# The first layer's up-projection by seven products of quarters, without the modulation vectors that nobody reads

## The chip, the cores and the metric

The kernel runs on one core of one Trainium2 chip, in one launch. The metric is the device time in microseconds (us). Five engines work side by side, each through its own list in its own order: TensorE (PE; the loads of its stationary operands are shown apart as PEld), VectorE (DVE), ScalarE (ACT), GpSimd (POOL) and SyncE (SP), which here issues the transfers of the weights. They wait for each other by semaphores.

## The reference, cut to what matters

Two layers of a transformer work on 512 tokens of x and 256 context tokens (ctx), 1024 features wide. Each layer has a mixer and then a feed-forward part, both behind a norm that is modulated by vectors computed from a conditioning vector, one set for x and one for ctx. After the second layer only x is returned, so that of ctx the second layer needs no more than what its mixer reads.

```python
hx = rmsnorm(x, g1) * (1 + sc1) + sh1          # and the same for ctx, with its own vectors
...                                            # mixer, output projection, gated residual
a, b = jnp.split(h @ w_up, 2, axis=-1)         # w_up: 1024 x 5632
return (jax.nn.silu(a) * b) @ w_down           # w_down: 2816 x 1024, then a gated residual
```

## The kernel before

Activations stand feature-major: a tile holds 128 features (partitions) by up to 768 tokens, x in columns 0 to 511 and ctx in 512 to 767. Every dense product of two float32 operands is made of three passes over float32r parts: each operand is split into a high part (a cast, on ACT, line 174) and a low part (operand minus high part, on VectorE, line 185); TensorE adds high·high, high·low and low·high. In the profile the tiles `whi` and `wlo` are the parts of weights, `act` the parts of activations, `t` temporaries, `main` and `bank` banks of PSUM.

**The up-projection.** The 22 feature tiles of the feed-forward part are taken in blocks (`F_BLOCKS`, line 27), six, six, six and four. The first two tiles of a layer come out of `Firsts` (line 725), which runs along with the norm, chunk by chunk of the contraction. For every other tile `f` the loop at line 1644 calls `dense_pass` (line 707) twice, for the half `a` that goes through silu and the half `b` that is multiplied: 8 chunks of contraction, three passes, once for 512 and once for 256 tokens. On layer 0 this is 96 matmuls a tile, 48 of 512 columns and 48 of 256. The result is taken out of PSUM by a silu on ACT and a product on VectorE, and split again, 512 and 256 wide. After each block comes the down-projection of its features, eight output tiles `m`, each added to the residual stream (`residual`).

**Weights** follow one list, `plan` (lines 350 to 489), which sets the order of loads, of splits and of uses. SP loads each item into one of four buffers `raw`. `w_next` (line 544) hands out the next item and lets `w_advance` (line 500) issue loads as buffers come free, and the split of the item ahead (cast and subtract, 1024 elements wide), into `whi` and `wlo`, two buffers each.

**Modulation items** stand in the same list. Those for the second half of layer 0's vectors and all of layer 1's are computed on VectorE beside dense products: `mod_step_v` (line 660) takes one item, two rows of 512 columns, by four instructions, two rows for each of x and ctx, and adds them up in two accumulators; after four items, two transposes, two reduces, a small product and an addition finish 512 modulation values for both. On layer 0 one item follows each half of each feature tile, one each down tile of the first three blocks, and two stand at the start of the feed-forward part, behind its first two tiles. The output projection's second half, `tail` at line 1594 with keys `o2` (the name in the list), has none.

**What sets the order.** Each engine runs its list in the order in which the program writes it; a rough clock per engine (`Plan`) decides where side chains (the norm, the transposes and reduces of modulation) are put between the main chain's instructions. `S.mm`, `S.tt`, `S.stt`, `S.acopy`, `S.act` are lines 136, 185, 196, 174 and 152; a profile's row names the helper's line.

Of the kernel before, what the change touches and what calls it, by code (L numbers as in the profile page):

```python
# [39 lines left out]
# a run of tokens: first, end, which modulation (x or ctx)  # L40
# [5 lines left out]
# column layout of the constant table  # L46
# [3 lines left out]
# column layout of the transposed small vectors  # L50
# [3 lines left out]
# column offsets of w_in  # L54
# [3 lines left out]
# fwd and bwd order of the 128-token tiles; tiles 4 and 5 are ctx  # L58
# [31 lines left out]
class Plan:  # L90
    """Keeps a rough clock per engine, so that independent chains of work are
    issued in an order in which the tensor engine seldom waits."""
# [33 lines left out]
    # -- the engines --  # L126
    def mm(self, out, lhsT, rhs, start, stop, tile_position=None):
# [7 lines left out]
        kw = {} if tile_position is None else dict(tile_position=tile_position)  # L135
        self.pin("pe", self.nc.tensor.matmul(out, lhsT, rhs, start=start, stop=stop, **kw))  # L136
# [5 lines left out]
    def behind(self, ins, other):  # L142
        # on one engine: the order of issue alone
# [15 lines left out]
    def preload(self):  # L159
        # one table that has both Exp and Ln  # L160
# [58 lines left out]
    # -- room in PSUM and SBUF, by the rough clock --  # L219
# [10 lines left out]
    def free(self, owner=None):  # L230
        # what is kept for a group of chains is free for that group alone
# [22 lines left out]
    # -- chains of work beside the main one --  # L254
# [62 lines left out]
def hybrid_kernel(ctx: ExitStack, tc: tile.TileContext, x, c, cx, c_ctx, w_mod, b_mod, norm1_g, norm2_g,  # L317
# [10 lines left out]
    # banks of PSUM: for the dense products, and for the chains beside them  # L328
# [22 lines left out]
    def w_item(key, n, load, width=P, hold=False):  # L351
        plan.append(dict(key=key, n=n, load=load, width=width, hold=hold, mod=False, early=False, read=False, late=False,
                         apart=False))

    # on the tensor engine up to the second norm, on the vector engine beside the first feed-forward part
# [3 lines left out]
    def mod_items(n):  # L359
        for _ in range(min(n, len(mod_todo))):  # L360
# [5 lines left out]
            else:  # L366
# [3 lines left out]
                             early=False, read=False))  # L370

    def first_mods(k):
        # shift and scale of the first norm, for the features of chunk k
# [80 lines left out]
    for l in range(DEPTH):  # L454
# [17 lines left out]
        for bi, (f0, f1) in enumerate(F_BLOCKS):  # L472
# [1246 lines left out]
```

## Time and profile before

| what | us |
|---|---|
| median of 3 runs | 1659.12 (1658.52 to 1661.16) |
| the profiled execution's span, first to last instruction | 1655.9 |
| time in it from which the output projection `o2` runs | about 390 |
| start of the up-projection's tiles after the first two | about 462 |
| end of layer 0's feed-forward part | about 981 |

The profiled execution's own time from outside is not listed; its span lies 3.2 us under the median of the runs. Rows of a window of the trace give, in this order, the stretch, its length, the busy time (and number of instructions) of PE, PEld, DVE, ACT and POOL, the granted clock as a share of full speed, the share of the 16 DMA engines and GB/s. Rows of a timeline give the start, the busy time of one row or of a run of equal ones, engine, line, operation, output and inputs, shapes and the count; a bracket at the end names the idle time ahead of it and what ended it. As instructions overlap at their ends, the pace of a stream is read from start to start, and not from the busy time.

### The profile page before, as it was taken

The page shows a single profiled execution, that of the slowest core. Times are in us where ns is not written, and L with a number is a line of the kernel's source. Part 1 is how long each engine was busy: PE and PEld are TensorE (multiplying, and loading weights), DVE is VectorE, ACT ScalarE, POOL GpSimd, SP SyncE. Part 2 cuts the span into 40 slices and gives each one's busy share as a digit, 9 for nine tenths or more (in the row PEclk, how much of TensorE's full clock was granted, in tenths as well). Part 3 has the DMA queues.
Part 4 walks back from the last instruction along what each step waited for, and adds up shares of the span by engine and source line. Part 5 has one row for each costly group of instructions (what it writes and reads, how often), then busy time and mean ns, then how long its engine had stood idle before and what let it go on. Part 6 is the DMA issues. An engine that isn't in the chain of part 4 may idle for free.

```text
span 1655.9 us, 26996 instructions
## 1 busy us (share of the span) xinstructions
PE 1619.7 (98%) x11021; PEld 1371.7 (83%) x11026; DVE 1056.2 (64%) x2016; ACT 598.7 (36%) x1194; POOL 35.7 (2%) x58
## 2 busy tenths in 40 slices
PE   7999999999999999999999999998999999999998
PEld 5878778888888888888888888786889888888887
DVE  5687877669867766767752366879787533333336
ACT  4454544543422122112212235555474422223224
POOL 2000000000000000000000000000000000000002
PEclk9999999999999999999999999999999999999999
DMA  9830312244234544444442152201123233232322
GB/s 259 253 100 15 90 52 77 83 160 138 67 115 124 145 125 121 138 128 140 127 118 71 33 146 52 64 27 52 65 77 90 77 89 106 83 117 84 100 85 77
DMA packets 252540, 168.45 MB, mean 102 GB/s; under 512 B 29700, under 2 KB 232960, under 8 KB 252416
## 3 DMA queue, kind: packets, MB, share of 16 engines
q1 hardware_dynamic: 248832, 155.93, 32.8%
q0 software_dynamic: 1760, 5.47, 1.1%
q10 hardware_dynamic: 1824, 5.31, 0.9%
q8 instruction: 87, 1.43, 0.4%
q14 instruction: 37, 0.30, 0.1%
HBM read 159.35 MB, written 7.34 MB: 101 GB/s over the span
## 4 chain that ended last, share of the span: by engine, by line
PE 83%; DVE 8%; ACT 2%; issue 1%; DMA 0%; SPq 0%; DVEq 0%; ACTq 0%
PE main L136 69%; PE bank L136 11%; DVE act L185 3%; PE bank L140 3%; DVE t L185 1%; DVE t L213 1%; ACT t L152 1%; DVE mx L204 1%; DVE wlo L185 1%; ACT t L174 0%; DVE t L190 0%; DMA raw<-in_w_mod_dram 0%; DVE t L196 0%; DVE t L1140 0%; DVE act L196 0%
## 5 line engine op out<-in xcount | busy, mean ns | idle before, releaser
L136 PE MATMUL main<-act,whi 128*128 128x512 f32 (+1 forms) x4160 | 1131.1, 357 | 1.3 <-ACT act L152 1.3
L136 PEld LDWEIGHTS main<-act,whi 128*128 128x128 f32 x4160 | 731.8, 189 | 115.2 <-issue 9.1
L136 PE MATMUL main<-act,wlo 128*128 128x512 f32 (+1 forms) x2080 | 735.8, 354 | 1.7 <-DVE wlo L185 1.7
L136 PEld LDWEIGHTS main<-act,wlo 128*128 128x128 f32 x2080 | 393.0, 189 | 57.5 <-issue 2.7
L174 ACT CAST whi<-raw 128x1024 fp32r<-128x1024 f32 (+3 forms) x194 | 189.9, 979 | 486.7 <-PE main L136 455.6
L185 DVE TENSOR_TENSOR wlo<-raw,whi 128x1024 fp32r<-128x1024 f32 (+3 forms) x194 | 219.4, 1131 | 181.7 <-ACT whi L174 178.9
L196 DVE SCALAR_TENSOR_TENSOR t<-raw,cst,t 128x512 f32<-128x512 f32 x210 | 148.3, 746 | 40.9 <-DMA raw<-in_w_mod_dram 40.5
L196 DVE SCALAR_TENSOR_TENSOR act<-main,mods,act 128x512 f32<-128x512 f32 (+1 forms) x160 | 97.8, 614 | 96.5 <-PE main L136 95.4
L185 DVE TENSOR_TENSOR t<-main,t 128x256 f32<-128x256 f32 (+1 forms) x73 | 43.9, 601 | 110.2 <-PE main L136 106.8
L174 ACT CAST act<-t 128x512 fp32r<-128x512 f32 (+3 forms) x102 | 61.0, 599 | 124.8 <-DVE t L185 124.3
L152 ACT ACTIVATE t<-bank,nm 128x256 f32<-128x256 f32 (+1 forms) x144 | 69.7, 496 | 60.2 <-DVE nm L196 55.5
L136 PE MATMUL main<-act 128*128 128x256 f32 (+1 forms) x576 | 88.6, 311 | 0.0
L136 PEld LDWEIGHTS main<-act 128*128 128x128 f32 x576 | 79.9, 191 | 6.1 <-issue 0.3
L185 DVE TENSOR_TENSOR act<-t,act 128x512 fp32r<-128x512 f32 (+5 forms) x110 | 73.6, 672 | 12.7 <-ACT act L174 10.5
L136 PE MATMUL bank<-act,whi 128*128 128x256 f32 (+3 forms) x336 | 74.9, 298 | 0.0
L152 ACT ACTIVATE t<-main 128x512 f32<-128x512 f32 x69 | 36.2, 525 | 88.9 <-PE main L136 88.7
L136 PE MATMUL bank<-act 64*64 64x64 f32 (+2 forms) x608 | 62.7, 273 | 3.6 <-DVE act L185 3.4
L185 DVE TENSOR_TENSOR act<-act 128x768 f32<-128x768 f32 (+7 forms) x84 | 64.7, 782 | 1.3 <-ACT t L174 1.1
L204 DVE TENSOR_REDUCE mx<-bank 128x2 f32<-128x512 f32 (+2 forms) x104 | 56.2, 561 | 14.2 <-PE bank L136 13.7
L140 PE MATMUL bank<-tab,t 128*128 128x128 f32 (+1 forms) x396 | 56.4, 277 | 4.1 <-DVE nm L196 1.7
L136 PE MATMUL bank<-t,t 128*64 128x128 f32 (+1 forms) x720 | 58.0, 283 | 1.7 <-DVE t L200 1.5
L136 PEld LDWEIGHTS bank<-act 64*64 64x64 f32 (+1 forms) x608 | 47.8, 161 | 12.9 <-issue 5.4
(133 smaller groups left out, 1208.7 us busy)
## 6 DMA issues: line engine op xcount, KB each, us to landing
raw<-in_w_mod_dram SPq DMA_DIRECT2D x92, 512.0 KB, 4.2
raw<-in_w_up_dram SPq DMA_DIRECT2D x80, 512.0 KB, 3.9
raw<-in_w_down_dram SPq DMA_DIRECT2D x48, 384.0 KB, 3.4
raw<-in_w_in_dram SPq DMA_DIRECT2D x26, 512.0 KB, 4.0
raw<-in_w_in_dram SPq DMA_DIRECT2D x16, 256.0 KB, 3.8
raw<-in_w_out_dram SPq DMA_DIRECT2D x16, 256.0 KB, 2.9
raw<-in_w_out_dram SPq DMA_DIRECT2D x32, 128.0 KB, 3.0
raw<-in_w_up_dram SPq DMA_DIRECT2D x16, 256.0 KB, 4.3
```

What stands on the lines that cost most here:

```text
L136: self.pin("pe", self.nc.tensor.matmul(out, lhsT, rhs, start=start, stop=stop, **kw))
L140: self.pin("pe", self.nc.tensor.transpose(out, in_, ident))
L152: ins = self.pin("act", self.nc.scalar.activation(out, in_, func, **kw))
L174: self.pin("act", self.nc.scalar.copy(out, in_))
L185: self.pin(eng, self._v(eng).tensor_tensor(out, a, b, op))
L196: self.pin(eng, self._v(eng).scalar_tensor_tensor(out, a, s, b, op0, op1))
L204: self.pin("dve", self.nc.vector.tensor_reduce(out, in_, AX.X, op))
L213: self.pin("dve", self.nc.vector.copy_predicated(out, mask, data))
```

## The change

For layer 0 the up-projection of tiles 2 to 21 is made by Winograd's form of Strassen's scheme. Its operands are cut in quarters: the weights by half (`a` in row 1, `b` in row 2) and by half of the contraction, `a11`, `a12`, `a21`, `a22`; the activations by half of the contraction and by half of the 768 tokens, `b11` to `b22`, 384 tokens wide. Seven products of quarters take the place of eight (table `SEVEN`); each is 4 chunks of contraction by three passes, 12 matmuls of 384 columns, and goes to PSUM in three banks, in which products that are added anyway share a bank. A `Unit` is one tile `f`: `make` forms the sums of weight quarters (four additions, three of them in the `raw` buffers themselves) and splits all seven operands, 512 elements wide each, and `after` takes the products out of PSUM and combines them. `run_units` sets the order; the product `p4` of a tile is run inside the next tile. Parts of weights are made at most four products ahead, in the four buffers that were `whi` and `wlo`.

The norm ahead of it, `Quartered`, keeps each chunk at full precision as well (one more ACT instruction for each) and makes sixteen differences of quarters, `t1` to `t4`, each split again. Layer 0's blocks become five (5, 5, 4, 4, 4 tiles), so there is one more round of eight down products. `Opened` starts a block's first two down products on all but their last tile of features, while that last tile is still being combined.

Modulation: of layer 1, from the third vector on, only x's are computed (`ni`), as nothing reads ctx's. The two items that stood at the start of the feed-forward part now follow the first tile of `o2`; the others are spread two to a feature tile up to the fourth tile and one after that, and by a table over the down tiles.

```diff
-F_BLOCKS = ((0, 6), (6, 12), (12, 18), (18, 22))
+F_BLOCKS = (((0, 5), (5, 10), (10, 14), (14, 18), (18, 22)), ((0, 6), (6, 12), (12, 18), (18, 22)))
...
+            if l == 0 and m == 0:
+                mod_items(2)
...
-            if l == 0 and bi == 0:
-                mod_items(2)
...
-                    if l == 0:
-                        mod_items(1)
...
+                if l == 0:
+                    mod_items(2 if f < 4 else 1)
...
-                if l == 0 and bi < len(F_BLOCKS) - 1:
-                    mod_items(1)
...
+                if l == 0 and bi < len(blocks) - 1:
+                    mod_items((0, 1, 2, 2, 1, 1, 1, 0)[m])
...
+            if at["split"] > i and plan[i]["quarters"] and not (it["mod"] or it["quarters"]):
+                break
...
     def mod_step_v(l, g, q):
+        ni = 1 if l == DEPTH - 1 and g >= 4 else 2
...
-            for a, i in zip(acc, range(2)):
+            for i, a in enumerate(acc):
...
+    class Opened:
...
+    class Quartered(Normed):
...
+        def split(self, name, kk, src):
+            hi, lo = self.at(name, kk)
+            S.acopy(hi, src)
+            S.tt(lo, src, hi.bitcast(F32), ALU.subtract)
...
+                S.act(full[:, t0:t1], full[:, t0:t1], AF.Identity, bias=B)
...
+        def differences(self, names):
...
+                    if name == "t1":
+                        d = h[:, left]
+                        S.tt(d, d, h[:, right], ALU.subtract)
...
+                    self.split(name, kk, d)
...
+    SEVEN = dict(p1=("a11", "b11", "v", True), p2=("a12", "b21", "q", True), p3=("s4", "b22", "r", False),
+                 p4=("a22", "t4", "v", False), p5=("s1", "t1", "r", True), p6=("s2", "t2", "v", False),
+                 p7=("s3", "t3", "v", False))
+    class Unit:
...
+        def make(self, name):
+            if self.raw is None:
+                mod_steps()
...
+            if name == "s1":
...
+                S.tt(src, R["a21"], R["a22"], ALU.add)
+            elif name == "s2":
+                S.tt(R["a21"], R["a11"], R["a21"], ALU.add)
+                src = R["a11"]
+                S.tt(src, R["a21"], R["a22"], ALU.add)
+            elif name == "s3":
+                src = R["a21"]
+            elif name == "s4":
+                src = R["a12"]
+                S.tt(src, R["a11"], src, ALU.add)
...
+            at["ring"] = 1 - at["ring"]
+            tag = ("whi", "wlo")[at["ring"]]
+            b = wp.tile([P, 1024], F32R, tag=tag, name=tag, bufs=2)
...
+            S.acopy(hi, src)
+            S.tt(lo, src, hi.bitcast(F32), ALU.subtract)
...
+            w_load()
+        def run(self, j):
...
+            hi, lo = self.parts.pop(wname)
+            for kk in range(4):
...
+                xh, xl = self.norm.at(xname, kk)
+                for i, (a, x) in enumerate(((hi, xh), (hi, xl), (lo, xh))):
+                    S.mm(pt, a[:, kk, :], x, first and kk + i == 0, kk == 3 and i == 2, more=not first)
...
+        def after(self, j, pt):
...
+            if j == "p1":
...
+                S.acopy(a1, pt)
+            elif j == "p2":
+                S.tt(a1, pt, a1, ALU.add)
...
+                S.act(a1, a1, AF.Silu)
+            elif j == "p5":
+                S.acopy(self.tb[:, :w], pt)
+            elif j in ("p3", "p6"):
+                if self.mid:
+                    S.tt(a2, pt, a2, ALU.add)
+                    S.act(a2, a2, AF.Silu)
+                else:
+                    S.acopy(a2, pt)
...
+            elif j == "p7":
+                S.tt(self.tb[:, :w], pt, self.tb[:, :w], ALU.add)
+            elif j == "p4":
+                S.stt(a1, pt, -1.0, a1, ALU.mult, ALU.mult)
...
+                S.stt(a2, self.tb[:, :w], -1.0, a2, ALU.mult, ALU.mult)
...
+                S.acopy(hi[:, :2 * w], self.ta[:, :2 * w])
+                S.tt(lo[:, :2 * w], self.ta[:, :2 * w], hi[:, :2 * w].bitcast(F32), ALU.subtract)
...
+    def run_units(units, made, then):
...
+            make += [(u, j) for j in ("p1", "p5", "p6", "p2", "p3", "p7", "p4")]
+            run += [(u, "p1"), (u, "p5"), *([(u - 1, "p4")] if u else []), (u, "p6")]
+            run += [(u, "p2"), (u, "p3"), (u, "p7")] if u < n - 1 else [(u, "p3"), (u, "p7"), (u, "p2")]
...
+            return i < 4 or make[i - 4] in ran
...
-                dense_pass([(m, *w_next(keys[m]), 0)], X, segs, ev_)
+                if m < len(opened):
+                    opened[m].close(ev_)
+                else:
+                    dense_pass([(m, *w_next(keys[m]), 0)], X, segs, ev_)
+                mod_steps()
...
+                run_units(units, 2, then)
...
+                opened = [Opened((0, *heads[0], 0), ts_, sg)]
+                opened.append(Opened((1, *w_next((l, "d", bi, 1)), 0), ts_, sg))
```

Three places show what moves in the engines' lists. The first is VectorE in `o2`. Output tiles of `o2` have their residual addition into `act_3941`, `act_3935` and so on, and the low part of the weights of tile m is the subtraction that reads `raw`; `t3` rows with `cst_144` are modulation. Before, the low parts of tiles 1, 2 and 3 (`act_4555`, `act_4596`, `act_4619`) follow one another:

```order
L196 SCALAR_TENSOR_TENSOR t3_4540<-raw_4453,cst_144,t3_4540 128x512
L196 SCALAR_TENSOR_TENSOR t3_4541<-raw_4453,cst_144,t3_4541 128x512
L185 TENSOR_TENSOR act_4555<-raw_4462,act_4555 128x512
L196 SCALAR_TENSOR_TENSOR act_3935<-main_4558,mods0_136,act_3935 128x512
L196 SCALAR_TENSOR_TENSOR act_3935<-main_4574,mods0_136,act_3935 128x256
L185 TENSOR_TENSOR act_4596<-raw_4542,act_4596 128x512
L209 STREAM_TRANSPOSE t3_4581<-t3_4291 128x512
L185 TENSOR_TENSOR act_4619<-raw_4549,act_4619 128x512
L204 TENSOR_REDUCE part_4539<-t3_4581 128x16
```

After, two modulation items (eight rows on `raw_4462` and `raw_4541`, with `raw_4462` now holding the first of them) stand between the low parts of tile 1 (`act_4553`) and of tile 2 (`act_4608`):

```order
L212 STREAM_TRANSPOSE t3_4579<-t3_4291 128x512
L199 SCALAR_TENSOR_TENSOR t3_4539<-raw_4462,cst_144,t3_4539 128x512
L188 TENSOR_TENSOR act_4553<-raw_4547,act_4553 128x512
L207 TENSOR_REDUCE part_4538<-t3_4579 128x16
L199 SCALAR_TENSOR_TENSOR t3_4540<-raw_4462,cst_144,t3_4540 128x512
L199 SCALAR_TENSOR_TENSOR t3_4539<-raw_4462,cst_144,t3_4539 128x512
L199 SCALAR_TENSOR_TENSOR t3_4540<-raw_4462,cst_144,t3_4540 128x512
L199 SCALAR_TENSOR_TENSOR t3_4539<-raw_4541,cst_144,t3_4539 128x512
L199 SCALAR_TENSOR_TENSOR t3_4540<-raw_4541,cst_144,t3_4540 128x512
L199 SCALAR_TENSOR_TENSOR t3_4539<-raw_4541,cst_144,t3_4539 128x512
L199 SCALAR_TENSOR_TENSOR t3_4540<-raw_4541,cst_144,t3_4540 128x512
L188 TENSOR_TENSOR act_4608<-raw_4550,act_4608 128x512
```

Eight rows now stand between the two low parts, a reduce and seven of the eight new modulation rows, and a transpose and the eighth stand ahead of tile 1's low part. Before, only tile 0's two residual additions stood between tile 1's and tile 2's.

The second place is VectorE early in the first block. Before, one feature tile needs the low parts of two weight items (`wlo`, 1024 wide), a product and a split for 512 and for 256 tokens, and the rest is modulation:

```order
L185 TENSOR_TENSOR t3_5248<-main_5323,t3_5248 128x512
L196 SCALAR_TENSOR_TENSOR t3_5383<-raw_5390,cst_144,t3_5383 128x512
L196 SCALAR_TENSOR_TENSOR t3_5382<-raw_5390,cst_144,t3_5382 128x512
L185 TENSOR_TENSOR act_5249<-t3_5248,act_5249 128x512
L185 TENSOR_TENSOR t3_5248<-main_5351,t3_5248 128x256
L196 SCALAR_TENSOR_TENSOR t3_5383<-raw_5390,cst_144,t3_5383 128x512
L185 TENSOR_TENSOR act_5249<-t3_5248,act_5249 128x256
L185 TENSOR_TENSOR wlo_5395<-raw_5317,whi_5394 128x1024
```

After, the same stretch holds the sums of weight quarters (`raw_5296`, `raw_5353`), subtractions of 512 for seven weight operands (out to `whi` or `wlo`, now one ring), the last differences of activations (`act_4938`, `act_4989`), the combination of the first tile (`t3_5290`, `main_5277`), and modulation's transposes and reduces:

```order
L188 TENSOR_TENSOR act_4938<-t3_5072,act_4938 128x384
L188 TENSOR_TENSOR raw_5353<-raw_5296,raw_5353 128x512
L212 STREAM_TRANSPOSE t3_5461<-t3_4540 128x512
L188 TENSOR_TENSOR raw_5296<-raw_5353 128x512
L207 TENSOR_REDUCE part_5378<-t3_5461 128x16
L199 SCALAR_TENSOR_TENSOR t3_5094<-t3_4990,t3_5094 128x384
L188 TENSOR_TENSOR whi_5448<-raw_5296,whi_5448 128x512
L199 SCALAR_TENSOR_TENSOR t3_5290<-t3_5318,t3_5290 128x384
L188 TENSOR_TENSOR act_4989<-t3_5094,act_4989 128x384
L188 TENSOR_TENSOR wlo_5505<-raw_5296,wlo_5505 128x512
L199 SCALAR_TENSOR_TENSOR t3_5290<-main_5277,t3_5290 128x384
L188 TENSOR_TENSOR raw_5296<-raw_5296 128x512
```

What were a few wide rows for a feature tile has become many narrower ones, and the norm's differences stand among them.

The third place is TensorE inside the first blocks. Before, a half's product is 8 chunks of 512 columns, then of 256 (here the end of one bank's 256 columns and the begin of the next bank's 512):

```order
L136 MATMUL main_5351<-act_5051,whi_5254 128x256 x2
L136 MATMUL main_5351<-act_5051,wlo_5255 128x256
L136 MATMUL main_5351<-act_5090,whi_5254 128x256 x2
L136 MATMUL main_5351<-act_5090,wlo_5255 128x256
L136 MATMUL main_5398<-act_4840,whi_5319 128x512 x2
L136 MATMUL main_5398<-act_4840,wlo_5320 128x512
L136 MATMUL main_5398<-act_4879,whi_5319 128x512 x2
L136 MATMUL main_5398<-act_4879,wlo_5320 128x512
```

After, every product is 384 wide: the second product of a tile (`bank_6308`), then the fourth of the tile before (`main_6173`), then the sixth (`main_6293`) and the second one by number (`bank_6370`):

```order
L139 MATMUL bank_6308<-act_5186,whi_6269 128x384 x6
L139 MATMUL bank_6308<-act_5306,whi_6269 128x384 x6
L139 MATMUL main_6173<-act_4852,whi_6228 128x384 x3
L139 MATMUL main_6173<-act_4898,whi_6228 128x384 x3
L139 MATMUL main_6173<-act_4938,whi_6228 128x384 x3
L139 MATMUL main_6173<-act_4989,whi_6228 128x384 x3
L139 MATMUL main_6293<-act_5324,wlo_6290 128x384 x6
L139 MATMUL main_6293<-act_5337,wlo_6290 128x384 x6
L139 MATMUL bank_6370<-act_5013,whi_6340 128x384 x3
L139 MATMUL bank_6370<-act_5031,whi_6340 128x384 x3
```

The previous tile's `p4` separates `p5` from `p6`, so that between `p6` and the following `p2` no other product stands.

More of the change, by code (lines that the diff above doesn't have):

```diff
@@ L546, in w_next @@
         assert it["key"] == key, (it["key"], key)
-        if at["use"]:
+        if at["use"] and not plan[at["use"] - 1]["quarters"]:
             plan[at["use"] - 1]["read"] = True
@@ new lines, in product_t, with there @@
+    def product_t():
+        if S.fits(dict(act=1)):
+            t = act_t(F32R)
+            return (t[:, 0], t[:, 1]), [t]
+        S.room(t3=2)
+        ts = [tmp(dt=F32R) for _ in range(2)]
+        return tuple(ts), ts
+    def run_units(units, made, then):
+        make, run = [], []
+        n = len(units)
+        for u in range(n):
+            make += [(u, j) for j in ("p1", "p5", "p6", "p2", "p3", "p7", "p4")]
+            run += [(u, "p1"), (u, "p5"), *([(u - 1, "p4")] if u else []), (u, "p6")]
+            run += [(u, "p2"), (u, "p3"), (u, "p7")] if u < n - 1 else [(u, "p3"), (u, "p7"), (u, "p2")]
+        run += [(n - 1, "p4")]
+        ran = set()
+        def there(i):
+            return i < 4 or make[i - 4] in ran
+        for r in run:
+            while made < len(make) and there(made):
+                v, j = make[made]
+                units[v].make(SEVEN[j][0])
+                made += 1
+            if made == len(make) and make[-4] in ran and make[-3] in ran:
+                then()
+                made += 1
+            units[r[0]].run(r[1])
+            ran.add(r)
+        if made == len(make):
+            then()
@@ L1637, in hybrid_kernel, with hook @@
                 evs = [swiglu(sil, act_t(F32R)) for sil in sils]
-                Firsts((l, "up"), (ga, gb)).run(norm, lambda i, s, pt: evs[i % 2]("ab"[i // 2], s, pt))
+                def hook():
+                    begin(range(2, f1))
+                if not last:
+                    diff = S.spawn(norm.differences(("t1", "t2", "t3")), prio=-1,
+                                   when=lambda: S.clk["pe"] if norm.done.get(gb, 0) == NK else None)
+                Firsts((l, "up"), (ga, gb)).run(norm, lambda i, s, pt: evs[i % 2]("ab"[i // 2], s, pt),
+                                                None if last else hook)
@@ L1639, in hybrid_kernel @@
                 S.gave(*sils)
+                if not last:
+                    S.spawn(norm.differences(("t4",)), prio=-1, when=lambda: diff["ready"] if diff["done"] else None)
+            if last:
                 X = norm.X()
-                mod_steps()
-            for f in range(max(f0, 2), f1):
-                S.room(t3=1, act=1)
-                sil = tmp()
-                ev_ab = swiglu(sil, act_t(F32R))
-                for nm in ("a", "b"):
-                    dense_pass([(nm, *w_next((l, nm, f)), 0)], X, sg, ev_ab)
-                    mod_steps()
-                S.gave(sil)
@@ new lines, in hybrid_kernel @@
+            if bi < len(blocks) - 1:
+                ev_d = lambda m, s, pt: residual(l, 5, pt, m, s)
+                for m in range(NK):
+                    if m < len(opened):
+                        opened[m].close(ev_d)
+                    else:
+                        w = (m, *w_next((l, "d", bi, m)), 0)
+                        if not last and m == NK - 1:
+                            begin(range(*blocks[bi + 1]))
+                        dense_pass([w], ts_, sg, ev_d)
+                    if m:
+                        mod_steps()
```

245 lines of the change are left out of this document (207 added, 38 removed).

## The prediction

> **What bounds the kernel now.** I read the page first: the busy times, and the chain that ended last by engine.
>
> ```profile
> span 1655.9 us, 26996 instructions
> PE 1619.7 (98%) x11021; PEld 1371.7 (83%) x11026; DVE 1056.2 (64%) x2016; ACT 598.7 (36%) x1194; POOL 35.7 (2%) x58
> PE 83%; DVE 8%; ACT 2%; issue 1%; DMA 0%; SPq 0%; DVEq 0%; ACTq 0%
> ```
>
> TensorE is busy for 98% of the span and carries 83% of the chain; VectorE has a third of its time left. An average hides stages, so the next view is the windows: the o2 and norm stage (384 to 462 us), 100 us of the up-projection, a down-projection, and the last stretch of layer 0's feed-forward part; then the waits of TensorE from 384 to 985 us, one row in all.
>
> ```profile
> 384.00:462.00 78.00, 76.81 (x453) 67.27 (x453) 65.70 (x122) 32.07 (x56) 0.00 (x0) 1.00 0.35 100
> 596.00:696.00 100.00, 100.00 (x596) 88.07 (x595) 66.94 (x106) 22.22 (x34) 0.00 (x0) 1.00 0.44 129
> 696.00:748.00 52.00, 52.00 (x311) 45.51 (x310) 38.62 (x62) 7.99 (x10) 0.00 (x0) 1.00 0.47 138
> 873.00:981.00 108.00, 108.00 (x623) 95.25 (x623) 41.91 (x62) 30.01 (x48) 3.41 (x7) 1.00 0.33 93
> PE bank L136 <- DVE t L185: 1.1, 1, 1.1
> ```
>
> In the stages that change TensorE never stands still, at a granted clock of 1.00. So matmul time taken out comes off the end, as long as the engines that feed it keep up. VectorE is the one to watch: 84% busy from 384 to 462 us, 67% in the up-projection. ACT (22%) and the DMAs (44%) have room.
>
> **What is removed.** The chain has the price of a feature tile, the timeline of TensorE that of one matmul.
>
> ```profile
> 595.77 33.55 PE main L136 x192
> 629.50 33.55 PE main L136 x192
> ...
> 385.88 0.63 PE L136 MATMUL main<-act,whi 128*128 128x512 f32 x2
> 388.62 0.40 PE L136 MATMUL main<-act,whi 128*128 128x256 f32 x2
> 390.06 0.63 PE L136 MATMUL main<-act,whi 128*128 128x512 f32 x2
> ...
> 267.80 0.51 PE L136 MATMUL bank<-act 128*128 128x384 f32 x2
> 268.15 0.23 PE L136 MATMUL bank<-trib,identb 128*128 128x128 bf16 x1
> ```
>
> 192 matmuls are two tiles, so a tile takes 33.55/2 = 16.78 us. Twelve matmuls of 512 run from 385.88 to 388.62 (0.228 each), twelve of 256 until 390.06 (0.120). Two of 384 take 268.15 − 267.80 = 0.35, 0.175 each, which is also the mean of 0.228 and 0.120. A tile by seven products is 84 of them: 14.70 us. Twenty tiles save 20 × (16.78 − 14.70) = **41.5 us**. The list of the changed kernel has 1680 matmuls of 384 more, 20 × 84, so the count is not in doubt.
>
> The Trainium skill, "TensorE: Matmul & The Clock Gate", section "Back-to-back issue gap", gives N/2.4 + 2.5 ns for a warm matmul of N columns alone. By that a tile would go from 15.6 us (48 of 512 and 48 of 256) to 13.65 (84 of 384), an estimated saving of 39 us in twenty; the rows lie about 12 ns above it at both widths, and the rows decide.
>
> **What is added on VectorE.** Its paces are read from start to start.
>
> ```profile
> 597.84 0.42 DVE L185 TENSOR_TENSOR t<-main,t 128x256 f32<-128x256 f32 x1
> 598.17 0.74 DVE L196 SCALAR_TENSOR_TENSOR t<-raw,cst,t 128x512 f32<-128x512 f32 x1
> 598.83 0.42 DVE L185 TENSOR_TENSOR act<-t,act 128x256 fp32r<-128x256 f32 x1
> 599.17 1.22 DVE L185 TENSOR_TENSOR wlo<-raw,whi 128x1024 fp32r<-128x1024 f32 x1
> 600.30 2.74 DVE L196 SCALAR_TENSOR_TENSOR t<-raw,cst,t 128x512 f32<-128x512 f32 x4
> ...
> 404.07 0.69 DVE L185 TENSOR_TENSOR t<-t,t 128x512 f32<-128x512 f32 x1
> 404.68 1.29 DVE L185 TENSOR_TENSOR act<-raw,act 128x512 fp32r<-128x512 f32 x2
> ```
>
> A two-operand row takes 0.33 at 256, 0.60 at 512 (404.07 to 404.68) and 1.13 at 1024; a modulation row 0.66 at 512. Between them by width: 0.47 for a two-operand row of 384, 0.87 for 768, 0.53 for a modulation-like row of 384. A tile needs four sums and seven low parts of 512 (11 × 0.60 = 6.6), three additions of 384 (1.4), two products (1.1) and the last subtraction (0.9): 9.9 us, where before two of 1024 and 0.60 + 0.33 twice made 4.1. One modulation item for both vectors is 4 × 0.66, with its share of transposes and reduces about 3.3 us; for x alone 1.6. By the order of the items, those for both end with the second block's down-projection. So a tile asks 13.2 us of VectorE's time in the second block and 11.5 in the last three, against 14.7 of TensorE's. On ACT seven casts of 512 at 0.62 and six rows up to 768 wide at no more than 0.93, by width, are under 10 us of 14.7:
>
> ```profile
> L174 ACT CAST act<-t 128x512 fp32r<-128x512 f32 x52 | 32.3, 621 | 109.7 <-DVE t L185 109.7
> ```
>
> The unread vectors take 56 modulation rows, 8 first rows, 8 transposes and 8 reduces off VectorE, about 50 us; since TensorE did not wait for it, this alone gains nothing, but it is the room in the last three blocks. The fifth block adds eight residual additions of each width (8 × 1.06 us) and no matmul; down stages then hold 40 of 42 us on VectorE in the first and 34 in the second. Both are hidden behind products; uncovered they would cost their 8.5 us.
>
> **Where TensorE will wait: o2.** Before, VectorE and TensorE stood like this:
>
> ```profile
> 392.77 0.74 DVE L196 SCALAR_TENSOR_TENSOR t<-raw,cst,t 128x512 f32<-128x512 f32 x1
> 393.43 0.69 DVE L185 TENSOR_TENSOR act<-raw,act 128x512 fp32r<-128x512 f32 x1
> 394.04 1.14 DVE L196 SCALAR_TENSOR_TENSOR act<-main,mods,act 128x512 f32<-128x512 f32 x2
> 395.09 0.68 DVE L185 TENSOR_TENSOR act<-raw,act 128x512 fp32r<-128x512 f32 x1
> ...
> 394.24 2.00 PE L136 MATMUL main<-act 128*128 128x512 f32 x8
> ```
>
> Tile 1's low part was done at 394.04, ahead of its product at 394.24. Now it comes behind tile 0's additions (until 395.09), a transpose and a modulation row, so at about 395.1 + 0.6 + 0.7 + 0.6 = 397.0, while the third matmul wants it at 394.7: 2.3 us. Tile 2's comes a reduce, seven modulation rows and itself later, 0.6 + 4.6 + 0.6 = 5.8 us, against a product of 12 × 0.228 = 2.7: another 3 us. Behind it VectorE is free again. I take **5 us**, with bounds 0, if VectorE comes to these rows early enough, and 8, all ten rows uncovered. The two loads moved ahead of o2's on SP cost nothing while the DMAs are at 35%.
>
> **Where it will wait: the first block.** The tiles began like this:
>
> ```profile
> 461.58 0.58 PE L136 MATMUL main<-act,whi 128*128 128x512 f32 x1
> ...
> 455.17 0.69 DVE L185 TENSOR_TENSOR t<-main,t 128x512 f32<-128x512 f32 x1 [3.45 <-ACT t L152]
> 459.77 1.22 DVE L185 TENSOR_TENSOR wlo<-raw,whi 128x1024 fp32r<-128x1024 f32 x1 [1.54 <-ACT whi L174]
> ```
>
> VectorE had 3.45 + 1.54 us to spare here, which the first operands and differences fill. From the first tile's first product to the third tile's, the new list gives VectorE 66 rows: 20 two-operand rows of 512 (12.0), 16 of 384 (7.5), 4 of 256 (1.3), one of 768 (0.9), 8 products of 384 (4.2), 10 modulation rows (6.6), 2 first rows (0.8), two transposes and two reduces (2.5) and a small one: 36 us. TensorE has 158 matmuls for it, 27.6 us. The difference, **8.4 us**, is a wait on low parts of weights. Bounds: 0 if the products could run ahead, which four part buffers forbid; 12 if the reduces also wait for their transposes.
>
> **The rest.** In the steady run the nearest hand-over is a12's: its part buffer comes free when the previous tile's p4 is done, and only p6 (12 × 0.175 = 2.1 us) lies between that and its use, for a cast of 0.62 and a subtraction of 0.6 to 0.7 that queue behind at most one other row. That leaves half a us. No row of before shows such a hand-over; the nearest is the one wait of 1.1 us above. With 17 steady hand-overs the bounds are 0 and 17 × 1.1 = 19 us; I take **4**, nearer to none, as the one row stands against forty tiles' halves without any.
>
> **Sum**, from the median 1659.1 (the profiled span lies 3.2 us below it, and what surrounds the span stays): 1659.1 − 41.5 + 5 + 8.4 + 4 = **1635 us**.
>
> **The rivals.** *The whole gain:* the waits are hidden by order; 1659.1 − 41.5 = 1617.6, up to 1627. For it: one wait row in 600 us; against: 36 us of rows over 27.6 of matmuls. 0.17. *More waits:* hand-overs and the first block at their upper ends, 8 + 12 + 19 = 39, so 1641 to 1657: 0.13, of which 0.03 lies within 0.2% of before. *384 columns at the pace of the weight load:*
>
> ```profile
> L136 PEld LDWEIGHTS main<-act,whi 128*128 128x128 f32 x4160 | 731.8, 189 | 115.2 <-issue 9.1 <-ACT act L152 1.9 <-DVE act L196 0.7
> ```
>
> At 0.189 a tile takes 15.9 us, the gain is 18 and the waits eat it: about 1659. Against it, 256 columns run at 0.120 under the same loads. 0.03. *Slower: VectorE sets the pace of every tile.* If rows of sums in the `raw` buffers, read and rewritten between loads, are drawn out so that a tile's rows come to 16.4 us instead of 13.2 and 11.5, TensorE waits 1.7 us in each of 20 tiles, 34 us, and the sum is 1659.1 − 41.5 + 13.4 + 34 = 1665. It decides from 28/20 = 1.4 us a tile, where the gain left by the two early waits is used up. For it: VectorE has only 1.5 us of room a tile in the second block; against: 67% busy without one wait. 0.11. *The clock falls back in a wait.* At the start TensorE waits and the clock does not:
>
> ```profile
> 0.00:10.00 10.00, 3.59 (x16) 3.14 (x16) 1.65 (x5) 3.98 (x7) 7.16 (x21) 1.00 0.74 220
> 30.00:60.00 30.00, 30.00 (x303) 24.92 (x301) 17.29 (x38) 10.19 (x19) 0.00 (x0) 1.00 0.86 218
> PE bank L140 <- DMA tab<-in_table_dram: 5.3, 1, 5.3
> ```
>
> After a gap of 5.3 us the granted clock is still 1.00. If it halved for some 3.4 us behind each of one to four longer gaps, the cost would be 2 to 7 us: 1637 to 1642. The Trainium skill, "TensorE: Matmul & The Clock Gate", section "Part 1: The HAM clock gate", has that rule (half rate after an idle window of about 3.4 us); this trace does not bear it out. 0.04.
>
> **How the numbers follow.** The forecast with waits of 10 to 24 us, 1627 to 1641, has 0.52. A measurement can tell about 0.2% from no change, 1655.8 to 1662.4. Faster: 0.52 + 0.17 + 0.10 + 0.04 = 0.83; same: 0.03 + 0.03 = 0.06; slower 0.11. The range goes from the whole gain to most of the case of more waits, 1617 to 1653, and leaves out some 0.19: 0.11 + 0.03 + 0.04 of the case of more waits + 0.01 below.
>
> **What would show it.** In the changed profile: tiles of about 14.7 us in blocks two to five and matmuls of 384 at 0.175; a wait of TensorE of about 5 us on low parts of o2 and of about 8 in the first block; VectorE some 90 us busier (20 × 5.8 for the tiles, 16 for the differences, 8.5 for the fifth block, less 50); no row of waits in the last three blocks. Wrong would be the forecast if weight parts are waited for in every tile, if 384 columns run slower beside this many other rows, or if the two early stages have no waits at all.

## The result and the profile after

| | us |
|---|---|
| before, median of 4 runs | 1658.82 (1657.87 to 1661.16) |
| after, median of 4 runs | 1633.98 (1632.20 to 1635.71) |
| ratio | 0.9848, 95% interval 0.9834 to 0.9862 |
| profiled execution after: its time, its span | 1632.85, 1630.9 |

The change makes the kernel 24.8 us faster; 1635 was forecast. First the page of the changed kernel, by the same three lines as before, and the waits of TensorE from the start of o2 to the end of layer 0's feed-forward part (engine, line and bank, who is waited for, total us, times, longest).

```profile
span 1630.9 us, 26988 instructions
PE 1586.0 (97%) x10786; PEld 1370.5 (84%) x10786; DVE 1149.9 (71%) x2212; ACT 681.1 (42%) x1374; POOL 35.8 (2%) x58
PE 79%; DVE 10%; ACT 2%; DMA 1%; issue 1%; SPq 0%; DVEq 0%; ACTq 0%
...
PE main L139 <- DVE wlo L188: 4.7, 4, 1.8
PE main L139 <- ACT act L177: 2.3, 2, 1.2
PE bank L139 <- ACT wlo L177: 2.2, 1, 2.2
PE main L139 <- DVE act L188: 1.5, 2, 1.0
PE main L139 <- ACT wlo L177: 1.1, 1, 1.1
PE bank L139 <- DVE wlo L188: 0.3, 1, 0.3
```

TensorE has 33.7 us less to do and VectorE 93.7 us more. Where one row of 1.1 us stood, six rows stand with 12.1 us, all of them on the parts of operands that VectorE and ACT make.

What a product costs is read from the timeline of TensorE in the third block:

```profile
682.90 2.24 PE L139 MATMUL main<-act,wlo 128*128 128x384 f32 x12
684.98 2.24 PE L139 MATMUL bank<-act,whi 128*128 128x384 f32 x12
```

Twelve matmuls of 384 take 2.08 us, 0.173 each; a tile of seven products is 14.56 us. The tile before, 48 × 0.228 + 48 × 0.120 = 16.7 us by its matmuls alone, had the small products of modulation besides (0.1 us of the chain's 16.78), which stay. Twenty tiles save 20 × (16.70 − 14.56), about 42.8 us. Of these 18.0 were given back. The places follow.

**o2**, TensorE and then VectorE:

```profile
395.92 0.73 PE L139 MATMUL main<-act 128*128 128x512 f32 x2 [1.21 <-ACT act L177]
397.15 2.99 PE L139 MATMUL main<-act 128*128 128x512 f32 x12 [0.49 <-DVE act L188]
401.25 0.73 PE L139 MATMUL main<-act 128*128 128x512 f32 x2 [1.11 <-ACT act L177]
402.98 4.23 PE L139 MATMUL main<-act 128*128 128x512 f32 x11 [0.99 <-DVE act L188]
...
396.41 0.69 DVE L188 TENSOR_TENSOR act<-raw,act 128x512 fp32r<-128x512 f32 x1
...
397.60 4.72 DVE L199 SCALAR_TENSOR_TENSOR t<-raw,cst,t 128x512 f32<-128x512 f32 x7
402.24 0.68 DVE L188 TENSOR_TENSOR act<-raw,act 128x512 fp32r<-128x512 f32 x1
```

The second tile's low part is done at 397.10 and the third's at 402.92, behind the seven modulation rows; TensorE waits 1.21 + 0.49 + 1.11 + 0.99 = 3.8 us. Two of these waits, 1.21 and 1.11 us, end with the cast of a high part on ACT, and the second of these casts had waited 2.52 us for its load: SP issues the rest of o2's weights from 391.75 us on, where the kernel before issued them in one run from 381.72 on. The low parts are done later still, so that VectorE's rows set the time here.

**The first block**, TensorE and two rows of VectorE:

```profile
483.94 0.61 PE L139 MATMUL bank<-act,wlo 128*128 128x384 f32 x2 [2.16 <-ACT wlo L177]
484.88 3.42 PE L139 MATMUL bank<-act,wlo 128*128 128x384 f32 x10 [0.33 <-DVE wlo L188]
500.45 0.62 PE L139 MATMUL main<-act,wlo 128*128 128x384 f32 x2 [1.05 <-ACT wlo L177]
502.85 2.02 PE L139 MATMUL main<-act,wlo 128*128 128x384 f32 x10 [1.78 <-DVE wlo L188]
...
496.81 5.38 DVE L199 SCALAR_TENSOR_TENSOR t<-raw,cst,t 128x512 f32<-128x512 f32 x8
502.11 0.68 DVE L188 TENSOR_TENSOR wlo<-raw,wlo 128x512 fp32r<-128x512 f32 x1
```

The waits of 5.3 us stand in the second tile (p5) and at the third tile's p1, whose low part follows eight modulation rows.

**The clock.** The windows of the two stretches:

```profile
400.00:420.00 20.00, 17.90 (x78) 13.98 (x78) 17.53 (x28) 8.69 (x13) 0.00 (x0) 0.91 0.66 195
480.00:500.00 20.00, 16.91 (x91) 15.35 (x89) 18.32 (x34) 8.15 (x17) 0.00 (x0) 0.91 0.21 66
```

The granted clock was 1.00 there before. In windows of 1 us it is 0.50 from about 402.7 to 406.1 and from 484.6 to 488.0: 3.4 us at half speed, each beginning within the second of two waits and costing up to 1.7 us. The rows above show it too: ten matmuls of 384 take 3.42 us at 484.88 and 2.02 at 502.85.

The second of these rows follows waits of 1.05 and 1.78 us, more than o2's last two, and yet no half clock follows it. The two stretches of half clock begin 81.9 us apart, 24 times 3.41. Windows of 3.41 us, counted from there, are these ahead of 402.66 and at the third tile's waits:

```profile
399.25:402.66 3.41, 1.62 (x6) 0.68 (x5) 3.41 (x6) 0.62 (x1) 0.00 (x0) 1.00 0.39 115
498.23:501.64 3.41, 1.78 (x9) 1.14 (x7) 3.41 (x6) 0.62 (x1) 0.00 (x0) 1.00 1.08 264
```

TensorE stands idle for 1.79 us in the first and for 1.63 in the second, as the border at 501.64 cuts the longer wait in two. Where a wait falls decides along with its length; the last section has the count over all profiles.

**The down stages.** At 746 us TensorE waits 1.7 us for a low part of the third tile's weights, at 841 1.0. VectorE, then the queue of loads:

```profile
746.33 0.49 DVE L193 TENSOR_SCALAR t<-raw,cst 128x512 f32<-128x512 f32 x1 [2.12 <-DMA raw<-in_w_mod_dram]
746.73 0.75 DVE L199 SCALAR_TENSOR_TENSOR act<-main,mods,act 128x512 f32<-128x512 f32 x1
747.39 0.68 DVE L188 TENSOR_TENSOR wlo<-raw,whi 128x512 fp32r<-128x512 f32 x1
...
741.20 1.94 SPq L519 DMA_DIRECT2D raw<-in_w_mod_dram  x2
```

VectorE has nothing to do, but its next row is a modulation row whose load was issued at 741.20 and has not landed; a residual addition and the low part are queued behind it.

### The profile page after: what moved, and what is told of

Read it like the earlier page. It is cut to its first block, busy times and chain, and to the rows that moved or that the text cites. A ratio compares the mean times of both kernels' runs of the same rounds, so it can differ in the third digit from the quotient of the medians.

```text
span 1630.9 us, 26988 instructions
## 1 busy us (share of the span) xinstructions
PE 1586.0 (97%) x10786; PEld 1370.5 (84%) x10786; DVE 1149.9 (71%) x2212; ACT 681.1 (42%) x1374; POOL 35.8 (2%) x58
## 4 chain that ended last, share of the span: by engine, by line
PE 79%; DVE 10%; ACT 2%; DMA 1%; issue 1%; SPq 0%; DVEq 0%; ACTq 0%
PE main L139 58%; PE bank L139 19%; DVE act L188 3%; PE bank L143 3%; DVE t L188 1%; DVE wlo L188 1%; DVE t L199 1%; ACT t L155 1%; DMA raw<-in_w_mod_dram 1%; DVE t L216 1%; ACT t L177 1%; DVE mx L207 1%; DVE t L193 0%; DMA raw<-in_w_out_dram 0%; ACT whi L177 0%
## 5 line engine op out<-in xcount | busy, mean ns | idle before, releaser
L139 PE MATMUL main<-act,whi 128*128 128x512 f32 (+2 forms) x2976 | 812.8, 364 | 1.8 <-ACT act L155 1.3
L139 PEld LDWEIGHTS main<-act,whi 128*128 128x128 f32 x2976 | 530.1, 189 | 83.7 <-issue 9.1
L139 PE MATMUL main<-act,wlo 128*128 128x512 f32 (+2 forms) x1728 | 547.3, 358 | 7.5 <-DVE wlo L188 6.5
L177 ACT CAST whi<-raw 128x1024 fp32r<-128x1024 f32 (+4 forms) x222 | 186.8, 841 | 426.8 <-PE main L139 357.8
L188 DVE TENSOR_TENSOR wlo<-raw,whi 128x1024 fp32r<-128x1024 f32 (+4 forms) x162 | 171.7, 1060 | 102.8 <-ACT whi L177 99.7
L139 PE MATMUL bank<-act,whi 128*128 128x384 f32 (+4 forms) x736 | 153.5, 319 | 0.0
L139 PE MATMUL bank<-act,wlo 128*128 128x384 f32 (+4 forms) x548 | 127.5, 328 | 2.5 <-ACT wlo L177 2.2
L139 PEld LDWEIGHTS bank<-act,whi 128*128 128x128 f32 (+1 forms) x736 | 124.5, 187 | 4.5 <-DVE whi L188 0.2
L139 PEld LDWEIGHTS bank<-act,wlo 128*128 128x128 f32 (+1 forms) x548 | 98.8, 189 | 6.1 <-ACT wlo L177 2.5
L139 PE MATMUL main<-t,whi 128*128 128x256 f32 (+1 forms) x296 | 74.3, 338 | 0.0
```

The source lines that it names most:

```text
L177: self.pin("act", self.nc.scalar.copy(out, in_))
L188: self.pin(eng, self._v(eng).tensor_tensor(out, a, b, op))
```

## The experiments

Each is timed together with the kernel before, on the same chip; the waits are from its profile. Stretches of half clock come and go from profile to profile also where an edit changes nothing (at 24 us the change has one and run 4 has none, at 500 us it is the other way round), at up to 1.7 us for each 3.4. So a difference of 2 to 3 us between two of the runs is weak by itself.

**1. The vectors dropped alone**, on the kernel before.

```diff
+        ni = 1 if l == DEPTH - 1 and g >= 4 else 2
...
-            for a, i in zip(acc, range(2)):
+            for i, a in enumerate(acc):
...
```

> The kernel before, with only the unread modulation vectors dropped: no product of quarters, blocks and places of items as before. Theory (TensorE did not wait for VectorE there, so 50 us less on VectorE are worth nothing by themselves): 1657 to 1660 us, the same as before. Rival (part of the gain of the change comes from the dropped vectors): 1653 us or less.

1659.13 us, ratio 1.0001 (0.9992 to 1.0010). VectorE is busy for 1011.4 us in the place of 1056.2 (44.8 less, where about 50 were estimated), and nothing is gained: TensorE did not wait for it.

**2. The vectors kept**, beside the seven products.

```diff
-        ni = 1 if l == DEPTH - 1 and g >= 4 else 2
+        ni = 2
...
-                ns = 1 if l == DEPTH - 1 and sc >= 2 else 2
+                ns = 2
```

> The changed kernel, but with the context's modulation vectors of layer 1 computed again from the third on, as before the change (about 50 us more on VectorE, none on TensorE). Theory (they are worth nothing while TensorE is the bound, but fill the down stages of the later blocks: eight items at 3.3 us and 13 us of other rows against 33.4 us of matmuls): the up-projection tiles of blocks three to five stay without waits at 13.2 of 14.6 us, and the down stages of the third and fourth block wait about 6 us each: 1644 to 1648 us. Rival (VectorE has room for them everywhere): 1633 to 1635 us. Second rival (the tiles wait too, as their rows come late by the order): above 1652 us.

1644.17 us, 10 us slower than the change. The waits of TensorE from 680 to 980 us, and the clock in two windows:

```profile
PE bank L139 <- DVE whi L188: 5.2, 2, 2.6
PE main L139 <- DVE wlo L188: 4.5, 6, 1.0
...
780.00:800.00 20.00, 18.29 (x102) 18.03 (x103) 18.09 (x31) 8.76 (x16) 0.00 (x0) 0.91 0.37 106
880.00:900.00 20.00, 17.84 (x92) 17.57 (x93) 17.24 (x31) 7.13 (x15) 0.00 (x0) 0.83 0.31 89
```

The time is as the theory had it, the place only half: 4.5 us in the down stages, 5.2 at the second product of the block behind each, and there the half clock besides. This profile also has half clock from 499 to 506 us, ahead of any row that the edit adds, so that not quite all of the difference is shown to be the vectors'. What is worth nothing alone is worth about 10 us beside the seven products.

**3. The two items put back** from o2 to the start of the feed-forward part.

```diff
-            if l == 0 and m == 0:
-                mod_items(2)
...
+            if l == 0 and bi == 0:
+                mod_items(2)
```

> The changed kernel, with the two modulation items that it has after the first tile of o2 put back to the start of the feed-forward part, behind the four weight loads of the first two tiles. Theory (VectorE's rows are the bound from the first up-projection tile to the third, and the eight rows cost their 5.3 us wherever TensorE has no cover for them): the wait of 3.8 us in o2 and the stretch of half clock behind it (1.7 us) go, and the waits in the first block rise from 6.0 us to about 11: 1632 to 1636 us, the same as the changed kernel. Rival (the wait in o2 is only a matter of place, and the start of the feed-forward part has room for the rows, as it had in the kernel before): the 5.5 us are simply gained, 1628 to 1629 us.

1628.37 us: the rival was right. The waits of TensorE from 389 to 980 us (one more is of 0.2 us); the window from the start of o2 to shortly behind the third tile's start, in the change (114 us) and here (107 us); and the window from the first tile's first product to the third tile's low part, in the change and here:

```profile
PE main L139 <- DVE wlo L188: 3.7, 4, 1.3
PE bank L139 <- ACT wlo L177: 3.6, 1, 3.6
PE bank L139 <- DVE t L188: 1.1, 1, 1.1
```
```profile
389.00:503.00 114.00, 104.89 (x594) 92.52 (x593) 105.05 (x197) 59.31 (x113) 0.00 (x0) 0.97 0.31 90
```
```profile
389.00:496.00 107.00, 100.95 (x582) 90.34 (x581) 102.60 (x196) 58.82 (x112) 0.00 (x0) 0.98 0.32 96
```
```profile
466.52:502.85 36.33, 31.02 (x169) 28.73 (x167) 34.63 (x66) 17.71 (x37) 0.00 (x0) 0.95 0.30 87
```
```profile
460.10:495.65 35.55, 30.66 (x169) 28.91 (x167) 35.52 (x68) 17.88 (x37) 0.00 (x0) 0.95 0.30 89
```

Within the first block the theory holds: VectorE is busy for all but 1.7 us of that stretch in the change and for all of it here. What it had wrong is the stage ahead, which had room. From the start of o2 on VectorE stands still for 9.0 us in the change and for 4.4 here: the wait in o2 held TensorE back, and VectorE then waited for TensorE's results, from 403 to 450 us for 4.7 us, 2.5 of them for o2's own products; in the same part of this run it is 2.1. So the rows that stood in o2 fit in later, ahead of the first block: TensorE's waits come to 8.6 us, where the change has 12.1, and the first block does not wait longer for having them ahead of it. With o2's half clock, which is gone too, that is about 5.2 of the 5.6 us.

**4. Products of zeros in o2's waits** (8 ahead of the second tile, 10 ahead of the third).

```diff
+                if l == 0 and which == 2 and m < 3:
+                    S.room(bank=1)
+                    zt = bank()
+                    for _ in range((8, 10)[m - 1]):
+                        S.mm(zt, zero[:, :P], zero, True, True)
+                    S.gave(zt)
```

> The changed kernel, with 8 and 10 products of zeros (512 columns, bfloat16, into a bank of their own that nothing reads) on TensorE ahead of o2's second and third tile, about as long as the waits there. Theory (the half clock seen for 3.4 us behind the third tile's wait comes from TensorE standing still): the third tile's product begins at the same time or a little later, the granted clock stays at 1.00 there, and 1.7 us are gained: 1632 us, and the window from 400 to 420 us shows a clock of 1.00 in the place of 0.91. Rival (the clock falls for another reason, or products of zeros do not count as work): a clock of 0.91 again and 1634 us.

1631.93 us. The window that had 0.91:

```profile
400.00:420.00 20.00, 19.59 (x100) 15.78 (x99) 17.58 (x29) 9.20 (x14) 0.00 (x0) 1.00 0.72 210
```

With TensorE kept busy, o2's waits fall from 3.8 us to 0.9, and the clock is 1.00 there. That the products of zeros did it is not shown by this: run 2 has o2's waits as in the change (3.8 us) and no such products, and its clock in the same window is 1.00 too:

```profile
400.00:420.00 20.00, 19.04 (x100) 15.58 (x100) 17.62 (x29) 9.07 (x14) 0.00 (x0) 1.00 0.70 209
```

Nor does the time decide. The medians lie 2.05 us apart, the runs overlap (1631.07 to 1633.02, 1632.20 to 1635.71), and the two profiles differ by a stretch of half clock at 24 us and one at 500 us as well.

**5. The early down items later.**

```diff
-                    mod_items((0, 1, 2, 2, 1, 1, 1, 0)[m])
+                    mod_items((0, 0, 2, 2, 2, 1, 1, 0)[m])
```

> The changed kernel, with no modulation item behind the second tile of each down-projection and one more behind the fifth (table 0, 0, 2, 2, 2, 1, 1, 0). Theory (at the start of the third and fourth block's down stage a modulation row stands at the head of VectorE's list and waits for its own load, and the low part of the third tile's weights is queued behind it): the waits of TensorE of 1.9 and 1.2 us there go, no others come: 1630 to 1632 us. Rival (the low parts are late by themselves, as all four raw buffers are taken): 1634 us, with the same waits on wlo.

1637.27 us, slower by 3.3 (1634.63 to 1638.85, against 1632.20 to 1635.71). VectorE in the third block's down stage:

```profile
747.53 1.54 DVE L199 SCALAR_TENSOR_TENSOR t<-raw,cst,t 128x512 f32<-128x512 f32 x2 [2.49 <-DMA raw<-in_w_mod_dram]
750.16 0.49 DVE L193 TENSOR_SCALAR t<-raw,cst 128x512 f32<-128x512 f32 x1 [1.09 <-DMA raw<-in_w_mod_dram]
...
751.22 0.68 DVE L188 TENSOR_TENSOR wlo<-raw,whi 128x512 fp32r<-128x512 f32 x1
```

With the item moved, other modulation rows meet loads that have not landed, ahead of the same low part, and TensorE waits longer (6.6 us on `wlo` of the `main` banks from 389 to 980 us, against 4.7); half clock follows the last of these waits, at 850 us. The theory's mechanism is there, but its cure was none: the loads are as late as the rival has it, and the wait moves to the next item.

**6. No early start of the down products.**

```diff
-                opened = [Opened((0, *heads[0], 0), ts_, sg)]
-                opened.append(Opened((1, *w_next((l, "d", bi, 1)), 0), ts_, sg))
+                opened = []
...
```

> The changed kernel without the early start of a block's first two down products: they run whole, after the last tile of features is combined. Theory (from the last product to the last tile's low part the trace has 3.3 us, of which the first tile's other chunks hide 2.1 us in blocks of four tiles and 2.7 in blocks of five): waits of about 1.0 us in each of three blocks and of 0.5 in two, together 4 us: 1637 to 1639 us. Rival (the early start hides nothing that the order of chunks did not hide before): 1634 us. Second rival (the parts of the weights come later too): 1642 us or more.

1631.38 us (1627.26 to 1634.26). The theory fell: the kernel is not slower than the change, rather 2.6 us faster, though the ranges overlap. The trace speaks for faster: of the waits at the down stages one of 0.3 us is left in the place of 2.9. The low part that was late with the early start comes in time without it; why was not tried apart, but the early start asks for two items of the list at once, and the modulation row that waits for its load then stands ahead of VectorE's next low part.

**7. Modulation rows left out.** Of the eight rows by which four items are added up, this kernel leaves out all but the first, for x and for ctx, from layer 0's sixth vector on; the loads stay.

```diff
-                else:
+                elif (l, g) < (0, 10):
```

> The changed kernel with VectorE's modulation rows left out from layer 0's sixth vector on, but for the first row of each four items and both vectors (the sums of these modulation vectors are left out; loads, transposes, reduces and the final additions stay). Theory (what TensorE gives back stands behind modulation rows on VectorE: 3.8 us in o2, 6.0 in the first block, two stretches of half clock of 1.7 each behind them, and 3.2 at two down stages): all of it goes, 1616 to 1619 us. Rival (sums, splits and differences of the seven products keep TensorE waiting in the first block by themselves): a wait of 3 us or more is left there and the time is 1621 to 1625 us.

1623.68 us, 5 us above the theory and in the rival's range, but not by the rival's cause. The waits in o2 and in the first block are gone without a rest, so the products' own sums and splits are not what TensorE waited for. What is left is four waits at the down stages, 5.5 us in all; one of them, VectorE's side and then TensorE's:

```profile
732.28 0.49 DVE L193 TENSOR_SCALAR t<-raw,cst 128x512 f32<-128x512 f32 x1 [3.83 <-DMA raw<-in_w_mod_dram]
...
734.15 1.13 DVE L199 SCALAR_TENSOR_TENSOR act<-main,mods,act 128x512 f32<-128x512 f32 x2
```
```profile
735.04 0.93 PE L139 MATMUL main<-act,whi 128*128 128x512 f32 x4 [2.07 <-DVE act L199]
```

VectorE, nearly empty, waits 3.83 us for a load, and the residual additions that free TensorE's banks stand behind it. There the bound is the load, not VectorE's work.

**8 to 10. The items spread anew.** None in o2, three in the first block instead of five, the last four of layer 0 in the first down stage, whose fifth tile waits for them; the rest two to a tile in the third and fourth block (8), or one to a tile and ten to a down stage (9); as 8 without the early start (10).

```diff
-            if l == 0 and m == 0:
-                mod_items(2)
...
-                    mod_items(2 if f < 4 else 1)
+                    mod_items((0, 0, 2, 1, 0, 1, 1, 1, 1, 1, 2, 2, 2, 2, 2, 2, 2, 2, 1, 1, 1, 1)[f])
...
-                    mod_items((0, 1, 2, 2, 1, 1, 1, 0)[m])
+                    mod_items(((0, 2, 2, 1, 1, 1, 1, 0), (0, 0, 2, 2, 2, 1, 1, 0), (0, 0, 2, 2, 2, 1, 1, 0), (0, 0, 2, 2, 2, 1, 1, 0))[bi][m])
...
+                    if l == 0 and bi == 0 and m == 4:
+                        S.wait(mod_now["task"])
...
```

> The changed kernel with its modulation items spread anew: none in o2, three in place of five in the first block, the last four of layer 0 behind the second and third tile of the first down stage (its fifth tile waits for them), two behind each tile of features in the third and fourth block, and none behind the second tile of the later down stages. Theory (VectorE's rows are the bound in the first block: two items less than with the items put back take 5.3 us off 36, so the waits of 5.7 us there and the half clock behind them go, and the 3 us at the down stages too): 1617 to 1621 us. Rival (two items to a tile make the next tile's weights wait for a raw buffer, as the load of the third tile's weights did, about 1 us in each of eight tiles): 1625 to 1629 us.

1620.79 us, ratio 0.9770 (0.9753 to 0.9787): 13 us less than the change, at the theory's upper end. The waits from 389 to 980 us:

```profile
PE main L139 <- DVE wlo L188: 1.9, 3, 1.0
PE bank L139 <- DVE part L207: 1.2, 1, 1.2
PE bank L139 <- ACT wlo L177: 0.6, 1, 0.6
```

3.7 us, and 0.2 elsewhere, are left of 12.1, and the clock is 1.00 from 400 to 420 and from 480 to 500 us.

> As the kernel before it in this set, but with one item behind each tile of features in the third and fourth block and ten, not seven, in each of the two down stages. Theory: 1617 to 1621 us, as no tile then has two items, and ten items at 1.6 us beside 13 us of other rows are under the 33.4 us of matmuls. Rival (the down stages become VectorE's or the loads' bound): waits of 1 to 3 us in each of two stages, 1621 to 1626 us.

1627.74 us (in the kernel before it a down stage had eight items, not seven): the rival named what came, though the time lies 1.7 us above its range. Four waits of 1.2 to 2.0 us stand right behind the two down stages, and two of 0.2 and 0.5 us in the first of them. Eight items left the tiles of the third and fourth block, four of them for the down stages and four for the last block's tiles, and 7 us were lost.

> The items spread as in the fastest kernel so far (none in o2, three in the first block, two to a tile in the third and fourth), and the first two down products of a block run whole instead of being started early. Theory (the early start hides nothing here either, and its only effect, loads and low parts that come late for the third tile, is already gone by the spread): 1619 to 1622 us, the same as with the early start. Rival (each of five blocks waits about 1 us for the last tile's combination, which the early start hid): 1624 to 1627 us. Second rival (the early start costs its 2.5 us here too): 1617 to 1619 us.

1620.75 us, as the theory had it: with loads in time the early start makes no difference to the time. The rival's wait for the last tile's combination is there, but at two down stages only (0.95 and 0.79 us).

## Why the prediction was right

- **The saving.** Forecast 41.5, measured 42.8. The step was sound; 384 columns cost 0.173, not 0.175, and the chain's tile held 0.1 us of products that stay.
- **o2.** Forecast 5 with 2.3 + 3; the low parts came at 397.10 and 402.92, and the waits are 3.8. The third tile's share was 2.1, as TensorE ended the second tile's part at 400.1, not at 399.3. The half clock behind it (up to 1.7) came on top, and a wait of 1.1 of before is gone: 4.4. The loads moved ahead, said to cost nothing, did put o2's further loads back to 391.75 us; that cost nothing only because the low parts came later still.
- **The first block.** Forecast 8.4, found 5.3 of waits and up to 1.7 of half clock: 7.0. Place and mechanism were right: 36 us of rows were forecast, and the stretch takes 36.3 us with VectorE busy for 34.6 of them. What was put too low is TensorE's share, 27.6 us; without waits and half clock it is 29.3. What such a sum doesn't tell is what the same rows cost a little earlier, where VectorE had idle time (run 3).
- **The rest.** Forecast 4. The hand-over at a12 on which it rested cost nothing in twenty tiles. What came in its place was 2.9 us at three down stages, 1.7 and 1.0 of them behind a modulation row waiting for its load at the head of VectorE's list, of which the prediction said nothing. VectorE came out 94 us busier, as worked out (90). A further 3.7 us, 18.0 − 4.4 − 7.0 − 2.9, were not followed up. They are not waits: TensorE is idle for 12.1 us from 389 to 980 us, which is the waits listed above.
- **Sum.** 42.8 − 18.0 = 24.8 us. So the total was right within 1 us, with errors of 0.6 to 2.6 us in its terms that cancel in part. That it came so close is luck.
- **The dropped vectors.** Said to gain nothing alone and to be the room for the last blocks: runs 1 and 2 show both.
- **The rivals.** The clock's falling back, given 0.04, happened in the stages that change, twice. The step that failed is the evidence chosen against it, a clock of 1.00 behind a first wait of 5.3 us at the start of the program. The rows of that stretch say otherwise: the trace has no record of the clock ahead of 11.6 us, and eight matmuls of one and the same shape take 1.97 us there and 1.07 later. The profile of before also has the case itself, further on:

```profile
8.38 1.97 PE L140 MATMUL bank<-tab,act 128*128 128x128 f32 x8 [1.13 <-DMA act<-in_x_dram]
14.30 1.07 PE L140 MATMUL bank<-tab,act 128*128 128x128 f32 x8 [0.47 <-DMA act<-in_ctx_dram]
...
1140.00:1160.00 20.00, 16.64 (x199) 12.38 (x200) 18.27 (x47) 10.12 (x28) 0.00 (x0) 0.83 0.10 27
...
1150.00 1.65 PE L140 MATMUL bank<-tab,t 128*128 128x128 f32 x10 [1.69 <-DVE nm L196]
1153.04 1.13 PE L136 MATMUL bank<-act,t 64*64 64x64 f32 x32 [1.39 <-ACT t L174]
```

The clock was 0.83 over these 20 us: 6.8 us at one half, from 1151.6 on, behind the first of the two waits and through the second. The other rivals did not come: 384 columns ran below the 0.189 of a weight load, and steady tiles had no waits.

## What to carry to other kernels

When a product is made cheaper, look at what the freed engine will wait for in the engines' order of rows: a few rows of side work ahead of an operand that is due cost most of their length (3.8 us of waits for eight rows of 0.66), and the same rows later cost nothing (run 3). A row whose load may be late should not stand ahead of an operand on an engine that works in order, not even on an idle one (run 7). Removing work from an engine off the critical path can be worth nothing by itself and still be worth about 10 us beside the next change (runs 1 and 2), and a spread of side work by the room of each stage was worth another 13 us.

## What the runs showed of the hardware

- Short waits can cost the clock, by where they fall. In the twelve profiles each stretch of half clock ahead of the last instructions lasts 3.41 or 6.83 us, and those of one profile begin whole multiples of 3.41 us apart. Of the windows so marked, from 14 us on and at full clock, all 27 in which TensorE is idle for 1.78 us or more are followed by half clock, and none with 1.63 us or less is; 4 of the 16 between are. TensorE's idle time is read from its rows, whose ends are modelled, so the border is no finer than that. The Trainium skill, "TensorE: Matmul & The Clock Gate", section "Part 1: The HAM clock gate", speaks of half rate after at least one idle window of about 3.4 us. The halving and its length agree with this trace; the idle time in front was shorter, and not without work.
- Whether products of zeros count as work for the clock is not shown by run 4, as run 2 has a clock of 1.00 there without them.
- A matmul of 384 columns keeps 0.173 us while the loads of its stationary operand take 0.189 each, so that these overlap each other.
